# Two padding tiles that shift where the tiles of a two-block fp32 network begin in SBUF

## The chip, the core and the metric

The kernel runs on one core of a Trainium2 chip. The metric is the time of one execution on the device in microseconds (us); it is given as the median of several executions. The core's engines are TensorE (PE: matrix multiplies, with its weight loads listed as PEld), VectorE (DVE), ScalarE (ACT), GpSimd (POOL) and SyncE (SP, which issues nearly all DMAs). They work in parallel and wait for one another through semaphores. SBUF is the on-chip memory that holds tiles: 128 partitions, and in each partition a range of bytes. A tile has one byte offset, which is the same in all of its partitions, and this study is about those offsets. PSUM is the memory that TensorE writes its sums to.

## What is computed

Two networks in a row, on one sequence of 256 tokens of width 1024, all in float32. The first has a stick-breaking attention layer and a forgetting attention layer, each followed by a gated FFN with a causal convolution of width 3; the second has a pooling layer and a latent-attention layer. Cut to the shapes that matter here:

```python
# first block, layer 0 and 1 (x: 1 x 256 x 1024, 16 heads of 64, D_FF = 2816)
a = rmsnorm(h, sb_pre_g);  q, k, v = split(a @ sb_w_qkv, 3)
h = h + rmsnorm(merge_heads(stick_breaking_attention(q, k, v)) @ sb_w_o, sb_post_g)
h = h + rmsnorm(conv_ffn(rmsnorm(h, ffn_pre_g[0]), w_up[0], conv_w[0], conv_b[0], w_down[0]), ffn_post_g[0])
...
o = forgetting_attention(q, k_sh, v_sh, fcum_sh)
h = h + rmsnorm(merge_heads(o) @ fox_w_o, fox_post_g)
h = h + rmsnorm(conv_ffn(rmsnorm(h, ffn_pre_g[1]), w_up[1], ...), ffn_post_g[1])
# second block
uz = rmsnorm_2(x, pool_norm) @ pool_w_in          # windowed means of u, silu(z), group matrices
x = x + (mixed * silu(z)) @ pool_w_out
proj = rmsnorm_2(x, mla_norm) @ mla_w_in          # q, kv latents, rope, gate z
x = x + (causal_mla_attention(...) * silu(z)) @ mla_w_out
return rmsnorm_2(x, final_norm)
```

## The kernel before

Every float32 operand of a product is split into a high and a low part of type fp32r (`split`, L64: ScalarE copies the high part, VectorE subtracts for the low part), and a product is three matmuls, high by high, high by low and low by high (`mm3`, L69; `mm3s`, L74, for several at once). Nearly all of TensorE's 6,955 matmuls are of this kind. A matmul names two operands in SBUF. The moving operand (`rhs`) is streamed column by column, mostly 256 or 512 columns; the stationary operand (`lhsT`), mostly 128 columns, is loaded beforehand by a weight load.

The weights come from HBM in chunks of up to 1 MB into tiles `raw` (pool rawp, 3 buffers, 8 KB per partition), issued by SyncE (`load_w`, L141). ScalarE and VectorE split them in parts of 1,024 columns into `wh` and `wl` (pools whp and wlp, 8 buffers each, 4 KB per partition; `bg_hi`, L157, and `bg_lo`, L173). The order of all work on each engine is written out by hand: `bg` calls between the matmuls place the splitting of later weights.

The stages run one after another. Names of the PSUM tiles tell them apart in the profile:

- `accV`: the values of the two attention layers (512 columns moving).
- `psq`: query and key projections (256 columns), with `z`, `po` and `accO` for logits, weighted values and output projection. `po` of the first block (`heads_out`, L527) has as operands `ph` and `pl`, the probabilities, and `vh` and `vl`, the values; `po` of the last layer (`pv`, L1203) likewise.
- `accS`, `psu`: the up-projections of the FFNs and the input projections of the pooling layer. `proj_A` (L407) multiplies a block of weights (stationary) by `aT`, the transposed activations (256 columns, moving).
- `accD`: the down-projections of the FFNs (weights moving, 512 columns; `gh`, `gl` stationary).
- `psg`, `accP`: the pooling layer's group matrices and output.
- `accL`, `psz`, `psr`, `psv`: the last layer. `psr` (`q_rope`, L1125) streams four pieces of 64 columns out of rows of 768; `psv` (`values`, L1182) four pieces of 128 columns out of rows of 1,024.
- `psf` (L836): the forget gates, with only 16 columns of weights, `wf`.
- `psT`, `pT`, `psn`, `pst`: transposes against the identity matrix `ident`, which is the moving operand.

Tiles lie in SBUF in the order in which their pools are opened (L41 to L49) and, in a pool, in the order in which the tiles are first asked for. The pools cst (`h`, `ident`, tables), rawp, whp, wlp, gp, nat, jk, sm and atp live for the whole kernel; the pools of a stage (sb, ff0, fx, pl, ml and so on) follow behind atp and share the space there. Tile sizes are multiples of 32 bytes after rounding. In the program this gives these offsets, in bytes per partition:

| tiles | begin at | past a multiple of 512 |
|---|---|---|
| cst: h, first tile of the pool | 16,512 | 128 |
| cst: ident | 24,704 | 128 |
| rawp, whp, wlp, gp, nat, jk | 27,744 and up, in steps of 4,096 or 8,192 | 96 |
| sm (rows of statistics) | 139,360 | mixed |
| atp: four aT tiles of 4,096 | 140,192 | 416 |
| operands in the pools of all stages behind atp (except `sel`, which stands 96 past) | 156,576 and up | 416 |

Within its tile an operand usually begins a multiple of 512 bytes further on (128 columns of 4 bytes). The exceptions are slices of the query weights of the last layer (steps of 768 bytes), rows of 320 columns in the latent projection (1,280 bytes), `wf` (64 bytes) and the broadcast column of `sel`.

Of the kernel before, what the change touches and what calls it, by code (L numbers as in the profile page):

```python
# [7 lines left out]
F32 = mybir.dt.float32  # L8
# [7 lines left out]
P = 128  # L16
# [11 lines left out]
TW = 1024  # L28
L3 = 384
WBUFS = 8  # L30
RAWB = 3
NLE_SET = 6

# [2 lines left out]
def tile_net(ctx: ExitStack, tc: tile.TileContext, t, out):  # L36
# [4 lines left out]
    cst = ctx.enter_context(tc.tile_pool(name="cst", bufs=1))  # L41
    rawp = ctx.enter_context(tc.tile_pool(name="rawp", bufs=RAWB))
    whp = ctx.enter_context(tc.tile_pool(name="whp", bufs=WBUFS))
    wlp = ctx.enter_context(tc.tile_pool(name="wlp", bufs=WBUFS))
    gp = ctx.enter_context(tc.tile_pool(name="gp", bufs=3))
    nat = ctx.enter_context(tc.tile_pool(name="nat", bufs=2))
    jk = ctx.enter_context(tc.tile_pool(name="jk", bufs=1))
    sm = ctx.enter_context(tc.tile_pool(name="sm", bufs=4))
    atp = ctx.enter_context(tc.tile_pool(name="atp", bufs=1))  # L49
    pacc = ctx.enter_context(tc.tile_pool(name="pacc", bufs=4, space=PSUM))  # L50
    pmm = ctx.enter_context(tc.tile_pool(name="pmm", bufs=4, space=PSUM))


    def hi_copy(hi, src, scale=1.0):
# [86 lines left out]
    def load_w(upto):  # L141
        while nxt["load"] <= min(upto, len(specs) - 1):
            v = specs[nxt["load"]][0]
            raw = rawp.tile([P, RAWW], F32, tag="raw", name="raw")
            rv = raw[:, :v.shape[1] * v.shape[2]].rearrange("p (a b) -> p a b", a=v.shape[1])

            for q in specs[nxt["load"]][1] if nxt["load"] < 2 else ():
                k0, k1 = parts[q]["cut"][0:2]
                nc.sync.dma_start(out=rv[:, k0:k1], in_=v[:, k0:k1])
                if q == 5:  # L150
                    load_x(1)
            if nxt["load"] >= 2:
                nc.sync.dma_start(out=rv, in_=v)
            loaded[nxt["load"]] = rv
            nxt["load"] += 1

    def bg_hi():  # L157

        n = nxt["hi"]
        if n >= len(parts) or (n >= WBUFS and parts[n - WBUFS]["used"] < parts[n - WBUFS]["need"]):  # L160
            return False
# [11 lines left out]
    def bg_lo():  # L173
        while nxt["lo"] < nxt["hi"]:
# [4 lines left out]
            if n == specs[q["chunk"]][1][-1]:  # L179
                load_w(q["chunk"] + RAWB)  # L180

# [119 lines left out]
    def gain(name, idx=None, g=None):  # L301
        src = t[name][idx] if idx is not None else t[name]
        n = src.shape[0]
        if g is None:
            g = gp.tile([P, D], F32, tag="g", name="g")[:, 0:n]
        nc.sync.dma_start(out=g, in_=src.unsqueeze(0).to_broadcast([P, n]))
        return g

    g_pre = gain("sb_pre_g", 0)
    load_w(RAWB - 1)  # L310

# [1138 lines left out]
```

## Time and profile before

| | us |
|---|---|
| median of 3 executions | 989.62 |
| lowest and highest of them | 987.88, 1492.68 |
| the profiled execution | 993.97 |
| its span, first to last instruction | 992.3 |
| TensorE busy in it | 976.6 |
| VectorE busy in it | 755.6 |
| ScalarE busy in it | 609.5 |
| GpSimd busy in it | 72.3 |

A profile page lists, engine by engine, the time in which at least one instruction was under way. Matmuls overlap: one starts before the one ahead of it has ended, so the mean duration of a matmul is a latency and says nothing of the rate. The rate is seen from start times, or from how many matmuls a stretch of known length holds. In the rows of the windows view the columns are: the stretch in us, its length, then busy us and the number of instructions for TensorE, its weight loads, VectorE, ScalarE and GpSimd, the granted clock of TensorE as a share, the share of DMA engines' time and GB/s. In timeline rows the columns are start in us, duration in us, engine, line, operation and tiles, and a count. In rows of groups: count, total busy us, mean ns of one, and idle time ahead of them.

### The profile page before, as it was taken

The page shows a single profiled execution, that of the slowest core. Times are in us where ns is not written, and L with a number is a line of the kernel's source. Part 1 is how long each engine was busy: PE and PEld are TensorE (multiplying, and loading weights), DVE is VectorE, ACT ScalarE, POOL GpSimd, SP SyncE. Part 2 cuts the span into 40 slices and gives each one's busy share as a digit, 9 for nine tenths or more (in the row PEclk, how much of TensorE's full clock was granted, in tenths as well). Part 3 has the DMA queues.
Part 4 walks back from the last instruction along what each step waited for, and adds up shares of the span by engine and source line. Part 5 has one row for each costly group of instructions (what it writes and reads, how often), then busy time and mean ns, then how long its engine had stood idle before and what let it go on. Part 6 is the DMA issues. An engine that isn't in the chain of part 4 may idle for free.

```text
span 992.3 us, 17580 instructions
## 1 busy us (share of the span) xinstructions
PE 976.6 (98%) x6955; PEld 900.1 (91%) x6955; DVE 755.6 (76%) x1299; ACT 609.5 (61%) x1050; POOL 72.3 (7%) x182
## 2 busy tenths in 40 slices
PE   8999999999999999999999999999999999999997
PEld 6899889999887899889999988899999899999996
DVE  5677788999945879977888873777767677887876
ACT  6489867667734657657666653565535455766663
POOL 1022220000001100020000000200000020110100
PEclk9999999999999999999999999999999999999999
DMA  8824346666572654525665565275565344544521
GB/s 297 262 86 149 128 136 209 208 225 201 179 246 85 214 171 149 170 86 174 200 222 183 200 234 190 63 248 207 186 211 187 114 126 136 199 156 146 159 101 42
DMA packets 116293, 170.79 MB, mean 172 GB/s; under 512 B 4227, under 2 KB 93683, under 8 KB 116211
## 3 DMA queue, kind: packets, MB, share of 16 engines
q1 hardware_dynamic: 116146, 169.68, 51.8%
q8 instruction: 54, 0.88, 0.4%
q14 instruction: 29, 0.23, 0.1%
q0 software_dynamic: 64, 0.00, 0.0%
HBM read 168.62 MB, written 1.05 MB: 171 GB/s over the span
## 4 chain that ended last, share of the span: by engine, by line
PE 92%; DVE 3%; ACT 2%; DMA 1%; POOL 1%; issue 1%; SPq 0%; POOLq 0%; DVEq 0%; ACTq 0%
PE psu L72 10%; PE psu L71 10%; PE psu L70 10%; PE accD L71 4%; PE accD L70 4%; PE accD L72 4%; PE psq L70 4%; PE psq L72 4%; PE psq L71 4%; PE accO L70 3%; PE accO L72 3%; PE accO L71 2%; PE accP L72 2%; PE accP L70 2%; PE accP L71 2%; PE accV L78 1%
## 5 line engine op out<-in xcount | busy, mean ns | idle before, releaser
L59 DVE TENSOR_TENSOR wl<-raw,wh 128x1024 fp32r<-128x1024 f32 (+3 forms) x300 | 352.5, 1197 | 92.4 <-ACT wh L55 89.6
L55 ACT ACTIVATE wh<-raw 128x1024 fp32r<-128x1024 f32 (+3 forms) x316 | 315.3, 1026 | 87.0 <-PE accD L72 32.8
L72 PE MATMUL psu<-aT,wl 128*128 128x256 f32 x864 | 240.4, 278 | 0.0
L70 PE MATMUL psu<-aT,wh 128*128 128x256 f32 x864 | 240.4, 278 | 0.0
L71 PE MATMUL psu<-aT,wh 128*128 128x256 f32 x864 | 240.2, 278 | 0.0
L71 PEld LDWEIGHTS psu<-aT,wh 128*128 128x128 f32 x864 | 162.2, 188 | 0.0
L70 PEld LDWEIGHTS psu<-aT,wh 128*128 128x128 f32 x864 | 162.0, 187 | 0.3 <-ACT zs L916 0.2
L72 PEld LDWEIGHTS psu<-aT,wl 128*128 128x128 f32 x864 | 162.1, 188 | 0.0
L703 DVE SCALAR_TENSOR_TENSOR yc<-psu,conv,yc 128x255 f32<-128x255 f32 (+1 forms) x160 | 73.5, 480 | 15.1 <-ACT yc L696 12.2
L70 PE MATMUL accD<-wh,gh 128*128 128x512 f32 x176 | 69.6, 396 | 0.0
L72 PE MATMUL accD<-wh,gl 128*128 128x512 f32 x176 | 69.5, 395 | 0.0
L71 PE MATMUL accD<-wl,gh 128*128 128x512 f32 x176 | 69.5, 395 | 0.0
L335 POOL TENSOR_TENSOR ss<-ss,epsc 128x1 f32<-128x1 f32 x24 | 11.9, 495 | 625.0 <-ACT junk L372 625.0
L696 ACT ACTIVATE yc<-psu,conv 128x256 f32<-128x256 f32 x80 | 40.8, 560 | 23.2 <-PE psu L72 23.1
L70 PE MATMUL psq<-aT,wh 128*128 128x256 f32 x192 | 54.1, 282 | 0.1
L71 PE MATMUL psq<-aT,wh 128*128 128x256 f32 x192 | 53.5, 279 | 0.0
L72 PE MATMUL psq<-aT,wl 128*128 128x256 f32 x192 | 53.5, 278 | 0.0
L708 ACT ACTIVATE yc<-yc 128x256 f32<-128x256 f32 x44 | 18.4, 418 | 48.7 <-DVE yc L703 48.7
L71 PEld LDWEIGHTS accD<-wl,gh 128*128 128x128 f32 x176 | 33.0, 188 | 8.1
L72 PEld LDWEIGHTS accD<-wh,gl 128*128 128x128 f32 x176 | 33.0, 188 | 8.0
L70 PEld LDWEIGHTS accD<-wh,gh 128*128 128x128 f32 x176 | 33.0, 188 | 7.9
L55 ACT ACTIVATE qkh<-psq 128x512 fp32r<-128x512 f32 x32 | 19.0, 593 | 32.4 <-PE psq L72 32.2
(334 smaller groups left out, 2277.0 us busy)
## 6 DMA issues: line engine op xcount, KB each, us to landing
raw<-in_w_up_dram SPq DMA_DIRECT2D x44, 1024.0 KB, 5.0
raw<-in_w_down_dram SPq DMA_DIRECT2D x22, 1024.0 KB, 5.2
raw<-in_pool_w_in_dram SPq DMA_DIRECT2D x16, 1024.0 KB, 8.2
raw<-in_sb_w_qkv_dram SPq DMA_DIRECT2D x10, 1024.0 KB, 6.2
raw<-in_w_kvf_dram SPq DMA_DIRECT2D x8, 1024.0 KB, 5.9
raw<-in_pool_w_out_dram SPq DMA_DIRECT2D x8, 1024.0 KB, 5.4
raw<-in_mla_w_in_dram SPq DMA_DIRECT2D x8, 1024.0 KB, 6.0
raw<-in_mla_w_out_dram SPq DMA_DIRECT2D x8, 1024.0 KB, 6.0
```

The costliest lines, as they stand in the source:

```text
L55: act.activation(out=hi, in_=src, func=AF.Copy, scale=scale)
L59: (eng or dve).tensor_tensor(out=lo, in0=src, in1=hi.bitcast(F32), op=ALU.subtract)
L70: pe.matmul(ps, lhsT=l[0], rhs=r[0], start=first, stop=False)
L71: pe.matmul(ps, lhsT=l[0], rhs=r[1], start=False, stop=False)
L72: pe.matmul(ps, lhsT=l[1], rhs=r[0], start=False, stop=last)
L78: pe.matmul(ps, lhsT=ls[m][0], rhs=rs[m][0], start=first and m == 0, stop=False)
L335: pool.tensor_tensor(out=s0, in0=s0, in1=epsc[:, 0:1], op=ALU.add)
L696: act.activation(out=y[:, u, :], in_=ps[:, u * S:(u + 1) * S], func=AF.Identity, bias=cp[:, 132 + q:133 + q], scale=cp[:, 88 + q:89 + q])
L703: dve.scalar_tensor_tensor(out=y[:, u, d:S], in0=ps[:, u * S:(u + 1) * S - d], scalar=w, in1=y[:, u, d:S], op0=ALU.mult, op1=ALU.add)
L708: act.activation(out=y[:, 0, :], in_=y[:, 0, :], func=AF.Gelu_apprx_tanh)
```

## The change

Two tiles are asked for right after the pools are opened, ahead of all others, and never written or read. The first, 232 columns of 4 bytes (928 bytes per partition), is in cst and comes to stand before `h`; the second, 48 columns (192 bytes), is in jk. All tiles behind them move by 928 or by 1,120 bytes. Instructions, their order and their waits are unchanged.

```diff
 WBUFS = 8
+PAD0 = 232
+PAD1 = 48
 RAWB = 3
...
     pmm = ctx.enter_context(tc.tile_pool(name="pmm", bufs=4, space=PSUM))
+
+
+    cst.tile([P, PAD0], F32, name="pad0")
+    jk.tile([P, PAD1], F32, tag="pad1", name="pad1")
```

## The prediction

> **What bounds the kernel now.** First the page's head, the busy table, the granted clock and the chain that ended last:
>
> ```profile
> span 992.3 us, 17580 instructions
> PE 976.6 (98%) x6955; PEld 900.1 (91%) x6955; DVE 755.6 (76%) x1299; ACT 609.5 (61%) x1050; POOL 72.3 (7%) x182
> ...
> PEclk9999999999999999999999999999999999999999
> ...
> PE 92%; DVE 3%; ACT 2%; DMA 1%; POOL 1%; issue 1%; SPq 0%; POOLq 0%; DVEq 0%; ACTq 0%
> ```
>
> TensorE is busy all the way, holds 92% of the chain, and its clock is not throttled. So only two things can move the time: how far apart consecutive matmuls start (I call that the pitch), and the 8% of the chain off TensorE. Next, the groups that cost most on it:
>
> ```profile
> L72 PE MATMUL psu<-aT,wl 128*128 128x256 f32 x864 | 240.4, 278 | 0.0
> ...
> L70 PE MATMUL accD<-wh,gh 128*128 128x512 f32 x176 | 69.6, 396 | 0.0
> ```
>
> The 278 and 396 ns are latencies that overlap. The pitch comes from counts in stretches that hold one kind of matmul: the up-projection of the first FFN, that of the second, and the down-projection of the first.
>
> ```profile
> 150.00:250.00 100.00, 100.00 (x884) 100.00 (x884) 90.42 (x146) 69.87 (x112) 0.00 (x0) 1.00 0.64 206
> 460.00:560.00 100.00, 100.00 (x851) 100.00 (x850) 86.90 (x142) 66.88 (x107) 0.00 (x0) 1.00 0.60 198
> 260.00:310.00 50.00, 50.00 (x216) 40.30 (x215) 27.85 (x32) 21.89 (x27) 0.19 (x1) 1.00 0.63 210
> ```
>
> A count includes the matmuls that stand over the left edge: latency by pitch, 2.4 for 256 columns and 1.7 for 512. So the pitch is 100/881.6 = 113.4 ns in the first FFN, 100/848.6 = 117.8 ns in the second, and 50/214.3 = 233.3 ns for 512 columns. This is the key observation. The two FFNs run the same code on the same four aT tiles (their tags in pool atp have one buffer each) and on the same weight rings, at the same addresses, yet one runs 4% slower per matmul. Two paces exist, and a given address does not decide which one a stretch gets. Counted start to start over the whole trace (the largest stretch of each kind is quoted above), 1,788 of the 256-column matmuls run at the fast pace, 2,937 at the slow one, and 1,368 matmuls have 512 columns.
>
> **The change part by part.** It adds no instruction, wait or DMA. What it moves is worked out from the order and sizes of the tiles. In each partition cst begins at byte 16,512, the weight pools rawp, whp and wlp begin 96 bytes past a multiple of 512, and atp and everything after it 416 past. The first pad is the first tile of cst, 928 bytes: 96 + 928 = 1,024, so whp, wlp, gp and nat come out at multiples of 512. The second adds 192 in jk: 416 + 928 + 192 = 1,536, so atp and all stage pools come out at multiples too. Three things do not: ident goes from 128 past to 32 past; the m_q slices step 768 bytes and so start 0 or 256 past; wf steps 64 bytes. In short, moving operands and weights go from "32 past a multiple of 64" to multiples of 512.
>
> Term 1, the pitch. The trace has no matmul whose operands both start at a multiple of 512, so I bound what a start address does by rows where addresses differ.
>
> Segmented operands. psr streams four pieces of 64 columns, 768 bytes apart, starting 96 or 352 past; psv streams four pieces of 128 columns 1,024 apart. Such streams touch more 512-byte blocks (6 against 3, and 8 against 5) and more 64-byte blocks (20 against 17, and 36 against 33) than a contiguous one.
>
> ```profile
> 894.28 0.28 PE L71 MATMUL psr<-wl,qTh 128*128 128x256 f32 x1
> ...
> 895.19 0.28 PE L70 MATMUL psr<-wh,qTh 128*128 128x256 f32 x1
> ...
> 909.59 0.40 PE L70 MATMUL psv<-wh,kTh 128*128 128x512 f32 x1
> ...
> 910.76 0.39 PE L72 MATMUL psv<-wh,kTl 128*128 128x512 f32 x1
> ```
>
> Eight steps of psr take 0.91 us, 113.8 ns; five of psv take 1.17, 234. To the rounding these are the contiguous paces. Were the pitch a cost per block touched, psr would need 20/17 of 113.4, 133 ns. So block crossings cost nothing that can be seen.
>
> Stationary operand. psf loads 16 columns, 64 bytes, in place of 128, from starts that step through the 512-byte block:
>
> ```profile
> 344.79 0.28 PE L71 MATMUL psf<-aT,wh 128*16 128x256 f32 x1
> ...
> 345.02 0.09 PEld L71 LDWEIGHTS psf<-aT,wh 128*16 128x16 f32 x1
> ...
> 345.69 0.28 PE L70 MATMUL psf<-aT,wh 128*16 128x256 f32 x1
> ```
>
> Eight steps in 0.90 us: 112.5 ns, the fast pace again, with an eighth of the weights read. The weight load, then, does not set the pitch, and neither does its start.
>
> The shape of the pitch. Twice the slow pace is 235.6, and 512 columns take 233.3: what a matmul pays once is about 2.3 ns, the rest grows with columns. A start address can spoil a stream's first block only, so what alignment could take from a matmul once is those 2.3 ns at most, 2.3 x 6,093 = 14 us if all of it went, and nothing says that it is due to the start. I take 0 for term 1, with ends from the paces: all 256-column matmuls at the fast pace, 2,937 x 4.4 ns = -12.9 us, or all at the slow one, 1,788 x 4.4 = +7.9 us. Both are reachable without any effect of alignment: a stretch appears to fall into a pace when the stream starts up.
>
> Term 2, transfers into raw tiles. Their destinations move from 96 past a multiple of 256 to multiples of it.
>
> ```profile
> 2.19 6.87 DMA raw<-in_sb_w_qkv_dram
> ...
> 853.83 4.78 DMA raw<-in_mla_w_out_dram
> ...
> raw<-in_w_up_dram SPq DMA_DIRECT2D x44, 1024.0 KB, 5.0
> ```
>
> The chain holds DMA for 1%, 9.9 us at most, nearly all in these two pieces; elsewhere a chunk lands in 5.0 us while a chunk lasts far longer on TensorE and three raw buffers run ahead. Gone altogether it would be -9.9; a like loss would be +9.9. No row shows an aligned transfer beside an unaligned one of the same kind, so I take 0, nearest to the hidden ones, and count 1 us each way.
>
> The Trainium skill (DMA: Bandwidth & Descriptors, "How a descriptor splits into AXI transactions") says that a read must start at a 256-byte boundary and that bytes before an unaligned start are fetched for nothing: 1,024 bytes from 96 would cost 35 beats in place of 32. Applied to these writes, which the page does not speak of, that is 9% of 9.9 us, an estimate of -0.9 us; no run here shows it, and the sum stays as it is.
>
> Term 3, ident, the moving operand of the transposes. The largest groups:
>
> ```profile
> L345 PE MATMUL psT<-ident,a 128*128 128x128 f32 x112 | 16.0, 276 | 3.7 <-DVE a L359 3.6
> ...
> L790 PE MATMUL pT<-ident,pt 128*128 128x128 f32 x96 | 13.2, 273 | 0.0
> ```
>
> With the smaller ones they are 284, and they would move to the other kind of start. If that cost them the 4% between the two paces, with a pitch of some 108 ns (below), it is 284 x 4.3 ns = +1.2 us; otherwise 0, which I take. VectorE and ScalarE keep instructions and shapes; in the densest stretch VectorE is busy 90.4 of 100 us beside a full TensorE, so changes there stay covered up to the missing 9.6%.
>
> Sum: 993.97 us (the profiled execution: span 992.3 and 1.67 around it) + 0 + 0 + 0. That execution stands 4.35 us above the median of the runs, 989.62. I predict the median, **989.6 us**, and for this case alone 976.7 to 997.5.
>
> **The rivals.** A, faster: the start address governs the pace, and aligned streams all run fast. For it: two paces are there, and no reason for the slow one is visible. Against it: one set of addresses gives both, and the psr, psv and psf rows. Price: 12.9 us for 256 columns; 512 would go to 2 x 113.4 - 2.3 = 224.5, 1,368 x 8.8 = 12.0; together -24.9, **964.7 us**. Its far end is the pitch of the transposes:
>
> ```profile
> 253.99 1.03 PE L465 MATMUL psn<-ident,xs 128*128 128x128 f32 x8
> ...
> L465 PE MATMUL psn<-ident,xs 128*128 128x128 f32 x24 | 3.1, 272 | 0.0
> ```
>
> Seven steps in 1.03 - 0.272 us: 108.3 ns, with an operand, ident, that does start at a multiple of 128. Should that be what 256 aligned columns cost: 2,937 x 9.5 + 1,788 x 5.1 + 1,368 x 16.7 = 59.8 us, 929.8. VectorE would still fit: its 90.4 us per 881.6 matmuls against 95.5. These are another kind of matmul, though, and each needs a full load of 128 columns.
>
> The Trainium skill (TensorE: Matmul & The Clock Gate, "Back-to-back issue gap") gives N/2.4 + 2.5 ns, 109.2 and 215.8; the trace disagrees for this stream (113.4 or 117.8, and 233.3). If alignment were what is missing, its figures would give an estimate of 57 us off.
>
> B, slower: before, the moving and the next stationary operand of most matmuls start at different places of a 512-byte block (416 and 96); after, at the same one, and the two reads collide. Rows in which both stand at 416 already:
>
> ```profile
> 106.41 0.40 PE L70 MATMUL po<-ph,vh 128*128 128x512 f32 x1
> ...
> 107.11 0.28 PE L70 MATMUL po<-ph,vh 128*128 128x256 f32 x1
> ...
> 889.94 0.28 PE L70 MATMUL po<-ph,vh 128*128 128x256 f32 x1
> ...
> 890.31 0.22 PE L70 MATMUL po<-ph,vh 128*128 128x128 f32 x1
> ```
>
> The first three take 0.70 us, 233.3 each, as everywhere: against it. The others take 0.37 us, 123.3 each: 5.5 over the slow pace, though in a run of three with 128-column matmuls around it. At 123.3 for all: 2,937 x 5.5 + 1,788 x 9.9 + 1,368 x 11 = 48.9 us, **1,038.5**. It decides (2%, 19.8 us) from 3.2 ns per matmul on.
>
> C, the change does not do what it says: ident and the m_q slices are not at multiples. That costs at most the 1.2 us above and stays in the forecast.
>
> **How the numbers follow.** Forecast 0.83, A 0.11, B 0.06. A bound of 2% is about what a measurement of this kernel can tell from no change: 969.8 and 1,009.4. A lies beyond the one, B beyond the other, the forecast's own ends within: faster 0.11, same 0.83, slower 0.06. The range holds the forecast's case to its ends, 1 us wider below for term 2 and rounded: 976 to 998; A and B, 0.17, are left out.
>
> **What would show it.** The window counts of the up-projections: 882 or 849 matmuls per 100 us net of edges and nothing else, 214 per 50 us in the down-projection. Right if both paces are still there, perhaps in other stretches. Wrong towards A if all 256-column stretches show 113 ns or less and 512 columns 225 or less; towards B if they show 120 or more. Term 2 is wrong if the first landing moves from 6.87 us by more than 1; term 3 if psn's eight transposes leave 1.03 us.

## The result and the profile after

The changed kernel takes 1003.07 us (median of 4 executions, 1001.74 to 1003.36) against 989.55 (987.88 to 989.62, and one execution of 1492.68 us, which the ratio leaves out); the ratio is 1.012, with a 95% interval of 1.009 to 1.015. It is slower by a little over 1%. The forecast was 989.6 us, with a range of 976 to 998. The profiled executions stand at 993.97 before and 1001.74 after.

The head, the busy table and the chain of the page of the changed kernel:

```profile
span 1000.0 us, 17580 instructions
PE 985.2 (99%) x6955; PEld 917.1 (92%) x6955; DVE 755.3 (76%) x1299; ACT 610.0 (61%) x1050; POOL 72.2 (7%) x182
...
PE 93%; DVE 2%; ACT 2%; POOL 1%; DMA 1%; issue 1%; SPq 0%; POOLq 0%; DVEq 0%; ACTq 0%
```

The instructions are the same, and VectorE, ScalarE and GpSimd are as busy as before to a microsecond. Only TensorE and its weight loads are longer. The groups that answer to those shown of before (lines have moved by 6):

```profile
L78 PE MATMUL psu<-aT,wl 128*128 128x256 f32 x864 | 244.5, 283 | 0.0
...
L76 PEld LDWEIGHTS psu<-aT,wh 128*128 128x128 f32 x864 | 165.9, 192 | 0.2
...
L76 PE MATMUL accD<-wh,gh 128*128 128x512 f32 x176 | 68.7, 390 | 0.0
```

The weight loads of before, for the second of these rows:

```profile
L70 PEld LDWEIGHTS psu<-aT,wh 128*128 128x128 f32 x864 | 162.0, 187 | 0.3 <-ACT zs L916 0.2
```

A matmul of 256 columns has become longer (283 ns against 278), and so has a weight load (162.0 us in 864 loads before, 187.5 ns each; 192 now), while one of 512 columns has become shorter (390 against 396). How this tells on the pitch is seen from the windows of the changed kernel: first and second up-projection, first down-projection.

```profile
150.00:250.00 100.00, 100.00 (x836) 100.00 (x835) 85.03 (x138) 65.27 (x105) 0.00 (x0) 1.00 0.59 193
460.00:560.00 100.00, 100.00 (x835) 100.00 (x835) 84.88 (x136) 65.78 (x104) 0.00 (x0) 1.00 0.60 201
265.00:315.00 50.00, 50.00 (x222) 41.44 (x221) 28.85 (x34) 23.30 (x31) 0.19 (x1) 1.00 0.62 211
```

With 2.4 and 1.7 matmuls taken off for the left edge, as before, that is 100/833.6 = 120.0 ns in both up-projections (113.4 and 117.8 before) and 50/220.3 = 227.0 in the down-projection (233.3 before). One count more or less is 0.1 ns in the first two and 1 ns in the third. The two paces of the 256-column matmuls of before are gone: the long streams all run at 120.0, slower than either. The long streams of 512 columns (accV, accO, accD, accP) all became faster.

Summed over the two traces from each start to the next, waits included, the 256-column matmuls on all 128 rows take 577.9 us instead of 561.5 (+16.4), the 512-column ones 318.4 instead of 326.1 (-7.7), everything else 1.0 less. The sum, +7.7, is the difference of the spans (1000.0 and 992.3). The medians differ by more, 13.5 us. Of that, some 4 us come from the profiled execution of before, which had the slow pace in its second FFN: a kernel with the same distances (e1 below) profiled with the fast pace there took 989.50 us, which is where the median of before lies. The profiled execution of after stands 1.3 us below its own median.

### The profile page after: what moved, and what is told of

The parts are those of the page before. It is cut to its first block, busy times and chain, and to the rows that moved or that the text cites. A ratio compares the mean times of both kernels' runs of the same rounds, so it can differ in the third digit from the quotient of the medians.

```text
span 1000.0 us, 17580 instructions
## 1 busy us (share of the span) xinstructions
PE 985.2 (99%) x6955; PEld 917.1 (92%) x6955; DVE 755.3 (76%) x1299; ACT 610.0 (61%) x1050; POOL 72.2 (7%) x182
## 4 chain that ended last, share of the span: by engine, by line
PE 93%; DVE 2%; ACT 2%; POOL 1%; DMA 1%; issue 1%; SPq 0%; POOLq 0%; DVEq 0%; ACTq 0%
PE psu L76 10%; PE psu L77 10%; PE psu L78 10%; PE psq L76 4%; PE psq L78 4%; PE accD L76 4%; PE accD L77 4%; PE accD L78 4%; PE psq L77 4%; PE accO L76 3%; PE accO L78 2%; PE accO L77 2%; PE accP L77 1%; PE accP L78 1%; PE accP L76 1%; PE accV L84 1%
## 5 line engine op out<-in xcount | busy, mean ns | idle before, releaser
L76 PE MATMUL psu<-aT,wh 128*128 128x256 f32 x864 | 244.7, 283 | 0.0
L77 PE MATMUL psu<-aT,wh 128*128 128x256 f32 x864 | 244.5, 283 | 0.0
L78 PE MATMUL psu<-aT,wl 128*128 128x256 f32 x864 | 244.5, 283 | 0.0
L76 PEld LDWEIGHTS psu<-aT,wh 128*128 128x128 f32 x864 | 165.9, 192 | 0.2
L77 PEld LDWEIGHTS psu<-aT,wh 128*128 128x128 f32 x864 | 165.9, 192 | 0.0
L78 PEld LDWEIGHTS psu<-aT,wl 128*128 128x128 f32 x864 | 165.9, 192 | 0.0
```

The costliest lines, as they stand in the source:

```text
L76: pe.matmul(ps, lhsT=l[0], rhs=r[0], start=first, stop=False)
L77: pe.matmul(ps, lhsT=l[0], rhs=r[1], start=False, stop=False)
L78: pe.matmul(ps, lhsT=l[1], rhs=r[0], start=False, stop=last)
```

## The experiments

All kernels below have only padding changed. Only two kinds of place matter for most matmuls: that of the weights (wh, wl) and that of the activations (atp and all stage pools behind it), each past a multiple of 512: 96 and 416 before, 0 and 0 after. "Distance" is activations less weights. Three theories stood at first. M: each stream counts by itself, and what counts is a start on a multiple of 64 bytes. R: the distance counts. W: only multiples of 512 act. In the fences that follow, the rows are windows of the kernel named: up-projection of the first FFN, in some also of the second, and the down-projection of the first FFN.

**e1: both places moved by 32 bytes.**

```diff
+    cst.tile([P, 8], F32, name="pad0")
```

> Weights begin 128 past a multiple of 512, activations 448: both multiples of 64, neither a multiple of 512, and the distance between them (320) is that of before. Theory M (what counts is whether a stream begins on a multiple of 64 bytes or 32 past one): pitches as after the change, 120.0 ns for 256 columns in both FFNs and 226.7 ns for 512, time about 1002 us. Theory R (what counts is the distance between the moving and the stationary operand in a 512-byte block): as before, 113.4 or 117.8 and 233.3, about 990 us. Theory W (only multiples of 512 do it): also as before, about 990 us.

Measured: 989.73 us, ratio 0.9985 (0.9968 to 1.0001).

```profile
150.00:250.00 100.00, 100.00 (x884) 100.00 (x884) 90.50 (x146) 69.80 (x112) 0.00 (x0) 1.00 0.63 206
460.00:560.00 100.00, 100.00 (x885) 100.00 (x884) 90.09 (x149) 69.14 (x110) 0.00 (x0) 1.00 0.62 205
265.00:315.00 50.00, 50.00 (x216) 40.07 (x215) 26.19 (x28) 21.72 (x29) 2.06 (x7) 1.00 0.57 189
```

The paces of before, 113.4 (in both FFNs here) and 233.3. M falls: the weights and activations are on multiples of 64, and nothing changed.

**e2: only the second tile of the change.** Weights and activations both at 96.

```diff
+    jk.tile([P, 48], F32, tag="pad1", name="pad1")
```

> Weights and activations both begin 96 past a multiple of 512: distance 0 as after the change, but 32 past a multiple of 64. M: as before, 113.4 or 117.8 and 233.3, about 990 us. R: as after, 120.0 and 226.7, about 1002 us. W: as before, about 990 us.

Measured: 1003.14 us, ratio 1.0115 (1.0087 to 1.0142).

```profile
150.00:250.00 100.00, 100.00 (x836) 100.00 (x835) 85.50 (x137) 65.73 (x106) 0.00 (x0) 1.00 0.60 195
...
265.00:315.00 50.00, 50.00 (x222) 41.42 (x221) 29.44 (x34) 23.34 (x30) 0.19 (x1) 1.00 0.62 211
```

The counts of the changed kernel to the last one, with neither weights nor activations on a multiple of 64. W falls too. The second tile of the change, which alone brings the distance to 0, has the whole effect.

**e3 and e4: one place at 0, the other 32 past a multiple of 64.** The tile in jk has 24 columns (96 bytes); e3 keeps the first pad, e4 leaves it out.

```diff
-PAD1 = 48
+PAD1 = 24
```

> Weights at 0, activations at 416 (32 past a multiple of 64). Most 256-column matmuls move activations against loaded weights, most 512-column ones move weights against loaded activations. M with the moving stream as the cause: 256 columns at 113.4 or 117.8, 512 at 226.7, about 990 - 9 = 981 us. M with the stationary operand as the cause: 256 columns at 120.0 and 512 at 233.3, about 990 + 18 = 1008 us. R: a distance of 96, no statement, but the same place for all matmuls of a kind. W: the stream that begins at 0 alone behaves as after.

> The other way round: weights at 96 (32 past a multiple of 64), activations at 0. M with the moving stream as the cause: 256 columns at 120.0, 512 at 233.3, about 1008 us. M with the stationary operand as the cause: 256 columns at 113.4 or 117.8, 512 at 226.7, about 981 us. If it takes both operands at multiples (W, or M for the pair), both this and the kernel with weights at 0 and activations at 416 show the pitches of before, about 990 us.

Measured: 1001.12 us, ratio 1.0092 (1.0064 to 1.0121), and 1001.95 us, ratio 1.0106 (1.0073 to 1.0139). First e3, then e4:

```profile
150.00:250.00 100.00, 100.00 (x855) 100.00 (x854) 87.14 (x143) 66.89 (x108) 0.00 (x0) 1.00 0.61 202
...
265.00:315.00 50.00, 50.00 (x216) 40.20 (x215) 27.14 (x31) 22.13 (x28) 0.94 (x3) 1.00 0.61 204
```

```profile
150.00:250.00 100.00, 100.00 (x855) 100.00 (x854) 87.07 (x141) 67.03 (x108) 0.00 (x0) 1.00 0.62 203
...
265.00:315.00 50.00, 50.00 (x216) 40.24 (x215) 27.39 (x32) 22.30 (x28) 0.33 (x2) 1.00 0.61 209
```

The two are mirror images in what begins where, and were to differ by 27 us under M. They show the same pitches, 117.3 and 233.3, which neither before nor after has. Their distances are 416 and -96, the same modulo 512. That is R again; the pitches of before, expected in case both operands had to be on multiples, did not come either.

**e5 to e8: the distance scanned.** Weights stay at 0; the tile in jk has 64, 80, 96 or 112 columns.

```diff
-PAD1 = 48
+PAD1 = 64    # e6: 80, e7: 96, e8: 112
```

> Weights at 0, activations at 64. Theory R, by now borne out: the distance of activations from weights decides; distance 0 gives 120.0 and 226.7 ns for 256 and 512 columns, 320 gives 113.4 or 117.8 and 233.3, 416 gives 117.3 and 233.3. Open is the length of the period. Period 128: 64 is the same as 320, so 113.4 or 117.8 and 233.3, about 990 us. Period 256: 64 is the same as 320 too. Period 512: a new place, no statement.

> Weights at 0, activations at 128. Period 128: the same as distance 0, 120.0 and 226.7, about 1002 us. Period 256 or 512: a new place, not 120.0 with 226.7. If collisions are what costs time, a place further from distance 0 should be no slower than before.

> Weights at 0, activations at 192. Period 128: the same as 64 and 320, 113.4 or 117.8 and 233.3, about 990 us. Period 256: a new place, the mirror of 64, so 256 columns and 512 columns change parts if only the size of the distance counts for the moving stream ahead or behind. Period 512: as at 320 with moving and stationary exchanged (192 = -320).

> Weights at 0, activations at 256. Period 128 or 256: the same as distance 0, 120.0 and 226.7, about 1002 us. Period 512: a new place, the farthest from distance 0; if the cost is a collision of two streams at the same place of a block, the lowest pitches are here, 113.4 or less and 226.7 or less, about 990 - 9 = 981 us or less.

Measured: e5 989.52 us, ratio 1.000 (0.9986 to 1.0013); e6 1003.64, 1.0135 (1.0105 to 1.0164); e7 986.94, 0.9972 (0.9938 to 1.0007); e8 1004.05, 1.0139 (1.0110 to 1.0168). In this order:

```profile
150.00:250.00 100.00, 100.00 (x885) 100.00 (x884) 90.50 (x147) 69.22 (x111) 0.00 (x0) 1.00 0.62 206
...
265.00:315.00 50.00, 50.00 (x216) 40.27 (x215) 26.19 (x28) 21.62 (x29) 2.06 (x7) 1.00 0.56 188
```

```profile
150.00:250.00 100.00, 100.00 (x845) 100.00 (x844) 86.23 (x139) 65.96 (x105) 0.00 (x0) 1.00 0.60 198
...
265.00:315.00 50.00, 50.00 (x216) 40.20 (x216) 28.13 (x32) 21.88 (x27) 0.19 (x1) 1.00 0.62 211
```

```profile
150.00:250.00 100.00, 100.00 (x884) 100.00 (x884) 90.34 (x146) 69.47 (x111) 0.00 (x0) 1.00 0.62 205
...
265.00:315.00 50.00, 50.00 (x220) 41.04 (x219) 27.11 (x29) 21.69 (x29) 2.02 (x7) 1.00 0.55 189
```

```profile
150.00:250.00 100.00, 100.00 (x836) 100.00 (x835) 85.30 (x137) 66.09 (x104) 0.00 (x0) 1.00 0.61 199
...
265.00:315.00 50.00, 50.00 (x222) 41.38 (x221) 30.69 (x36) 24.66 (x31) 0.19 (x1) 1.00 0.64 215
```

Distance 256 is distance 0 again, and 64 is 320: the period is 256 bytes or a part of it, and since 128 is neither (118.7 and 233.3) it is 256. The hope that the place farthest from distance 0 is the best one did not come true. Distance 192 is a little better than before in its pitches, 113.4 for 256 columns and 229.0 for 512; the interval of its time still holds 1.

**e9: one pair of operands alone.** If the distance is what counts, the down-projection can be changed without touching anything else.

```diff
+            fg.tile([P, 48], F32, name="padg")
             gT = [fg.tile([P, NF, S], F32R, name=n) for n in ("gh", "gl")]
```

> The kernel before, with 192 bytes of padding ahead of gh and gl alone: these two, the stationary operands of accD, come to 96 past a multiple of 512, the same as the weights; all other operands stay where they were. Theory R (the distance between the two operands of a matmul's stream and load, period 256): accD alone goes from 233.3 to 226.7 ns, 528 matmuls, 3.5 us less in the two down-projections, every other pitch as before, about 987 us. Rival S (the layout as a whole, such as the distance of all pools from one another or where the weight rings lie, decides): accD stays at 233.3, about 990 us.

Measured: 986.36 us, ratio 0.9956 (0.9939 to 0.9973). The third row is that of the down-projection, which begins earlier here:

```profile
150.00:250.00 100.00, 100.00 (x885) 100.00 (x884) 90.20 (x145) 70.16 (x112) 0.00 (x0) 1.00 0.64 208
460.00:560.00 100.00, 100.00 (x852) 100.00 (x851) 86.92 (x142) 67.15 (x107) 0.00 (x0) 1.00 0.59 193
...
258.00:308.00 50.00, 50.00 (x222) 41.42 (x221) 30.07 (x35) 23.95 (x31) 0.19 (x1) 1.00 0.62 212
```

The down-projection goes to 50/220.3 = 227.0 ns; accO, accP and accV stay at 233.3 to 233.4 start to start, and the up-projections keep the two paces of before. The saving of the medians is 3.6 us against the expected 3.5, though the paces of the 256-column streams alone scatter by as much; the pitch is the firmer evidence. For accD the cause is the pair of operands, not the layout as a whole. Nor does its pace hang on what the other engines do meanwhile: the few steps of accD in the first down-projection during which VectorE, ScalarE and GpSimd were all idle average 226.6 ns here (16 steps) and 226.6 in the changed kernel (13), the others 226.7 and 226.8.

**e10: the low weights alone moved by 64 bytes,** to see which of the loads slows which matmul.

```diff
+    wlp.tile([P, 16], F32, tag="padw", name="padw", bufs=1)
-PAD1 = 48
+PAD1 = 32
```

> The changed kernel with the low weights wl alone moved by 64 bytes: wh and the activations at distance 0, wl and the activations at 192 (mod 256). In the up-projections the three matmuls of a step load wh, wh, wl. Theory N (a matmul is slowed by the load that runs beside it, that of the next matmul): the pitch behind the middle matmul of the three, beside which wl is loaded, falls to 113 to 118 ns, the other two stay at 120.0. Theory O (a matmul is slowed by its own load): the pitch behind the third matmul falls. If a pace is a property of the whole stream, all three change together.

Measured, in a single execution: 998.54 us.

```profile
150.00:250.00 100.00, 100.00 (x852) 100.00 (x851) 86.91 (x141) 66.50 (x107) 0.00 (x0) 1.00 0.61 201
...
265.00:315.00 50.00, 50.00 (x217) 40.48 (x216) 27.67 (x31) 22.26 (x28) 0.78 (x3) 1.00 0.61 208
```

The whole stream went to 100/849.6 = 117.7 ns; start to start the mean pitch behind the three matmuls of a step is 117.5, 117.5 and 118.3. Neither N nor O shows: one operand of three at another distance sets all three. The groups of its weight loads:

```profile
L79 PEld LDWEIGHTS psu<-aT,wl 128*128 128x128 f32 x864 | 165.9, 192 | 0.0
L78 PEld LDWEIGHTS psu<-aT,wh 128*128 128x128 f32 x864 | 162.5, 188 | 0.0
```

The loads of wl take the 192 ns that all loads of psu take in the changed kernel, though wl is the one that is no longer at distance 0 from the activations; those of wh, which still is, take 188. So the length of a load does not follow its own distance, and which load runs into which stream is not settled.

**e11 and e12: distances of 224 and 32,** to see whether the pitch changes in steps of 64 bytes (PAD1 of 104 and 56).

> Weights at 0, activations at 224, 32 short of distance 0 by the period of 256. At 192 the pitches are 113.3 or 117.8 for 256 columns and 228.9 for 512. If the pitch changes in steps of 64 bytes this is one of its two neighbours (113.3 to 118 with 229, about 987 us, or 120.0 with 226.7, about 1003 us); if it changes smoothly, 117 with 228, about 995 us.

> Weights at 0, activations at 32. Between distance 0 (120.0, 226.7) and 64 (113.3 or 117.8, 233.3). By steps of 64 bytes one of the two, 1003 or 990 us; smoothly, 118 and 230, about 996 us.

Measured: 1002.67 us, ratio 1.0127 (1.0107 to 1.0147), and 996.95 us, ratio 1.0069 (1.0049 to 1.0090). First e11, then e12:

```profile
150.00:250.00 100.00, 100.00 (x848) 100.00 (x847) 86.09 (x139) 67.20 (x106) 0.00 (x0) 1.00 0.61 200
...
265.00:315.00 50.00, 50.00 (x216) 40.18 (x215) 28.75 (x33) 22.52 (x29) 0.19 (x1) 1.00 0.63 211
```

```profile
150.00:250.00 100.00, 100.00 (x860) 100.00 (x859) 87.75 (x143) 67.37 (x108) 0.00 (x0) 1.00 0.61 204
...
265.00:315.00 50.00, 50.00 (x216) 40.23 (x216) 27.16 (x31) 22.16 (x28) 0.94 (x3) 1.00 0.60 204
```

Neither a step nor a smooth change: 118.3 and 116.6 ns for 256 columns, and in both 233.3 for 512, though one neighbour of each has 227. Odd multiples of 32 are places of their own. The times alone would have misled: 1002.67 and 996.95 us are what a step to distance 0 and a smooth change had been expected to give.

The two kernels also show that the distance has a sign. accS multiplies the same tiles by 256 columns at a time, but with the weights moving and the activations stationary. Start to start it runs at 116.7 ns in e11 and 118.3 in e12, where psu runs at 118.3 and 116.7. So what counts is moving less stationary operand: 224 for psu and 32 for accS in e11, the other way round in e12.

**e13 and e14: two distances in one kernel.** Of the distances tried, the 256-column stages are fastest at 64 or 192, the 512-column ones at 0. Both can be had, since e9 shows that pairs can be set singly. The same padding is put ahead of gh, of oTh in both attention layers, and of yh in the pooling and the last layer: 16 columns on top of e7 (e13), 48 columns on top of the kernel before (e14).

```diff
+            fg.tile([P, 16], F32, name="padg")      # e14: 48 here and below
             gT = [fg.tile([P, NF, S], F32R, name=n) for n in ("gh", "gl")]
...
+        sbv.tile([P, 16], F32, name="pado")
         oT = [sbv.tile([P, KD, S], F32R, name=n) for n in ("oTh", "oTl")]
...
+            if g == 0:
+                pl_.tile([P, 16], F32, tag="pady", name="pady", bufs=1)
             yT = [pl_.tile([P, 4, S], F32R, tag=n, name=n) for n in ("yh", "yl")]
```

> Weights at 0, activations at 192 as in e7, but gh, gl, oTh, oTl, yh, yl and the latents' kT at distance 0 from the weights. Theory R, pair by pair: psu, psq and psz at the pitches of e7 (113.3, in some stretches 117.8), accD, accP at 226.8 to 227.1 and accO about 228, accV unchanged at 229.4, psq against kT at 120 (96 matmuls); e7's 987 us less 528 x 2.1 + 360 x 2.1 + 192 x 2.9 ns = 2.4 us, about 984.5 us, 0.6% below before. Rival S (the layout as a whole): one of these groups does not follow, about 987 us.

> The kernel before with the same stationary operands alone brought to 96 past a multiple of 512, where the weights are. Theory R: psu, psq, psz as before (113.3 or 117.8 by stretch), accV 233.3, accD 226.8, accP 227.1, accO 228.3; before less 528 x 6.5 + 360 x 5.1 + 192 x 6.3 + 48 x 4 ns = 6.7 us, about 983.5 us, 0.7% below before. Rival S: accO and accP stay at 233.4, 987 us as with gh and gl alone.

Measured, beside 994.10 us for the kernel before on the same chip: e13 981.97 us, ratio 0.9893 (0.9869 to 0.9917); e14 985.13 us, ratio 0.9916 (0.9896 to 0.9936). First e13, then e14:

```profile
150.00:250.00 100.00, 100.00 (x885) 100.00 (x884) 90.32 (x147) 69.34 (x111) 0.00 (x0) 1.00 0.62 205
460.00:560.00 100.00, 100.00 (x851) 100.00 (x850) 87.29 (x142) 66.15 (x107) 0.00 (x0) 1.00 0.58 191
...
258.00:308.00 50.00, 50.00 (x223) 41.40 (x221) 29.35 (x34) 23.33 (x30) 0.19 (x1) 1.00 0.63 211
```

```profile
150.00:250.00 100.00, 100.00 (x885) 100.00 (x884) 90.37 (x146) 69.99 (x112) 0.00 (x0) 1.00 0.64 206
460.00:560.00 100.00, 100.00 (x884) 100.00 (x884) 90.24 (x148) 70.07 (x112) 0.00 (x0) 1.00 0.61 200
...
258.00:308.00 50.00, 50.00 (x223) 41.39 (x222) 29.81 (x34) 23.56 (x30) 0.19 (x1) 1.00 0.63 211
```

Every group that was to gain went where R puts it: accD 226.8 in both, accP 226.8 and 227.2, accO 228.4 and 228.3 (steps over 250 ns left out), with accV at 229.2 and 233.3 as in e7 and before. Rival S falls. The times are 1.1% and 0.8% below before, where 0.6% and 0.7% were expected.

One thing was not foreseen. The pad in the last layer's pool also moves the pool behind it, with qT, kT and rTh. All 240 query and key matmuls of the last layer (psq), not only the 96 against kT, went to 119 to 120 ns, from 114 to 115 before; R says so too, since qT is now at distance 0 as well. Against before it costs both kernels some 240 x 5 ns = 1.2 us.

The second up-projection of e13 ran at the slow pace in this execution and that of e14 at the fast one, so the paddings do not settle which of the two paces a stretch takes. e13 is the fastest kernel of the study, some 1% below the kernel before and 2% below the changed one by the ratios.

## Why the prediction was wrong

**What bounds the kernel** was right, and so was the reading that the pitch decides: the steps of the 256- and 512-column matmuls make +8.7 us of a difference of +7.7 between the spans, everything else -1.0.

**Term 1, the pitch, is the step that failed.** The prediction took 0 because "block crossings cost nothing that can be seen", "the weight load, then, does not set the pitch, and neither does its start", and because a start address "can spoil a stream's first block only". Each looked at one stream by itself, and a single stream's place indeed does nothing: e1 moves every start, keeps the distances, and runs as before; e2 moves no weight, brings the distance to 0, and runs as the changed kernel. What was missed is the distance between the two operands. It comes to 0 by the change, and that costs 256 columns 2.2 to 6.6 ns a matmul and gives 512 columns 6.3 back: +16.4 and -7.7 us in place of 0. The 2.3 ns that were to bound any gain came from the slow pace; twice the fast pace is 226.8, 6.5 below the 233.3 of 512 columns, and it is about there that distance 0 puts them.

The rows of psr and psv could not have shown it. The pieces of psr begin 96 and 352 past a multiple of 512, which looks like two places but is one modulo 256; psv's pieces step 1,024. Both keep the distance of every other weight. The row of psf did hold other distances: its weights step by 64 bytes, so its matmuls run through distances 64, 0, 192 and 128 in turn, and the stream settles at 113.3 ns over all four. But its loads have 16 columns, and it does not speak for loads of 128. The remark that one set of addresses gives both paces was right, yet it shows only that 64 (modulo 256) is a distance with two paces, not that distances are alike.

**Rival B named the right quantity, and was dismissed on a row too short.** It said that two operands at the same place of a block collide, and was set aside because three 512-column matmuls of po, both at 416, ran at 233.3 "as everywhere". In the changed kernel a stream takes some matmuls to reach its pace. The timeline of accV after a stall:

```profile
322.58 0.40 PE L85 MATMUL accV<-wl,aT 128*128 128x512 f32 x1
...
323.75 0.40 PE L84 MATMUL accV<-wh,aT 128*128 128x512 f32 x1
...
325.14 0.39 PE L84 MATMUL accV<-wh,aT 128*128 128x512 f32 x1
...
325.82 0.39 PE L85 MATMUL accV<-wl,aT 128*128 128x512 f32 x1
```

Five steps from 322.58 to 323.75 are 234 ns each; three from 325.14 on are 227. Three matmuls do not tell. A longer stream with both operands at 416 stood in the trace of before: ten matmuls of 256 columns in the logits of the last layer.

```profile
915.47 0.28 PE L70 MATMUL z<-qkh 128*128 128x256 f32 x1
...
916.31 0.40 PE L70 MATMUL accO<-wh,yh 128*128 128x512 f32 x1
```

Seven steps take 0.84 us, 120.0 ns each: the pitch that the change then brought to the other streams. Over the six streams of this kind the steps from the fifth on average 119.4 ns, in the changed kernel too, where their distance is 0 as well. B's price was wrong in the other part too: 123.3 for 256 columns was taken from a run of three among others, the steady value is 120.0, and for 512 columns the sign is the opposite one, which a plain collision does not explain. So B's 1,038.5 was far too high, and the time ended within 2%, between the forecast and B.

**Term 2**: 0, give or take 1 us, was right. The first landing of the changed kernel, against 6.87 us before:

```profile
2.19 6.22 DMA raw<-in_sb_w_qkv_dram
```

That is 0.65 us less, but the start of raw is not shown to be the reason. With raw at a multiple of 512 as well, the same landing took 6.45 us in e3, 6.77 in e5, 6.93 in e10 and 7.42 in e12, on both sides of the 6.87 that it took with raw at 96 past one (before and e2). So the estimate of 0.9 us that was worked out from the Trainium skill (DMA: Bandwidth & Descriptors, "How a descriptor splits into AXI transactions") is not borne out: the landings scatter by more than that, and no run moves raw alone. **Term 3**: psn's eight transposes take 1.03 us as before; 0 was right.

**Rival A** fell: in the changed kernel no long 256-column stream came near 113; the streams that begin at multiples of 512 run at 120.0. **Rival C** carries no weight: the transposes against ident kept their time, and e2 has the whole effect with neither weights nor activations on a multiple of 512. The end of +7.9 us for "all at the slow pace" was too low because there is a pace beyond it.

## What to carry to other kernels

Where TensorE sets the time, take the pitch from start times, stage by stage, and compare stages that run the same code; a pitch that differs between kinds of matmul is worth a scan of paddings, which costs nothing but a few hundred bytes. What counted here, with loads of 128 columns, is not where an operand begins but how far apart, modulo 256 bytes, the moving and the stationary operand begin, and the best distance differs with the number of moving columns. At distance 0, accS and accV, which both move weights against loaded activations, went opposite ways: accS, with 256 columns, to 119.7 ns (113.6 to 117.7 before), accV, with 512, from 233.3 to 228.0. A pad ahead of single tiles sets a stage by itself, but it also moves what lies behind it. A row that is to rule out a steady effect must hold a steady stream, and a row with another address is a test only if the quantity in question is another one there.

## What was not expected of the hardware

The pitch of a matmul of fp32r operands with a weight load of 128 columns beside it, by the distance of activations from weights, modulo 256 bytes (256 columns: psu of the up-projections, activations moving; 512: first down-projection, weights moving, so that moving less stationary is 256 less the number in the first column; from the windows above, 512 columns to 1 ns). The rows hold for these two streams; accS of 256 columns, weights moving, runs at 119.9 in e3 and e4, where moving less stationary is 96.

| activations less weights | kernels | 256 columns, ns | 512 columns, ns |
|---|---|---|---|
| 0 | after, e2, e8 | 120.0 | 227.0 |
| 32 | e12 | 116.6 | 233.3 |
| 64 | before, e1, e5 | 113.4 or 117.8 | 233.3 |
| 128 | e6 | 118.7 | 233.3 |
| 160 | e3, e4 | 117.3 | 233.3 |
| 192 | e7 | 113.4 or 117.8 | 229.0 |
| 224 | e11 | 118.3 | 233.3 |

At distances 64 and 192 each up-projection ran at one of two paces from its first blocks to its last, and the same kernel can show the one in the first FFN and the other in the second. What picks the pace is open. The 959 steps of psu in an up-projection at 4.4 ns are 4.2 us. Some kernels at these distances scatter by that much (e1: 987.93 to 993.19), though not all (e5: 988.97 to 990.41), and those at distance 0 hardly (e2: 1002.64 to 1003.36).

The Trainium skill (TensorE: Matmul & The Clock Gate, "Step-by-step: what each phase is for") says that TensorE reads the moving and the stationary operand through two independent ports and that loading the next weights takes no read bandwidth from the running matmul. The measurements show that the two are not independent here: the pitch follows their distance, and at distance 0 the loads of the up-projections take 192 ns in place of 187.5. That the two reads meet in some part of the memory that repeats every 256 bytes is the obvious reading, but no run shows the part itself, and the loads of e10 do not fit the simplest form of it. Nor does R cover loads of 16 columns. psf runs through the same four distances before and after the change, only beginning its round at another one, and yet its mean pitch went from 113.8 to 117.1 ns. What collides, if anything does, stays open.
